# A hybrid decoder layer on one core: modulation columns summed one turn after their load is issued

## The chip, the core and the metric

The kernel runs on one core of one Trainium2 chip. The metric is the device time of one execution in microseconds (us). Times of before are three runs; a profile of one further execution shows where its time went. The core has TensorE (PE, matrix products), VectorE (DVE), ScalarE (ACT), GpSimd (POOL) and SyncE (SP), which here issues all loads and stores from one queue.

## The reference

One layer on 256 tokens of width 2048, all in 32-bit floats. The condition `c` gives nine modulation vectors of 2048 each, three (shift, scale, gate) for each of three parts:

```python
cond = jax.nn.silu(c)
mod = cond @ ada_w[l] + ada_b[l]
sh1, sc1, gt1, sh2, sc2, gt2, sh3, sc3, gt3 = jnp.split(mod, N_MOD, axis=-1)
h = ada_in(x, norm_g[l, 0], sh1, sc1)
x = x + MACARON_W * gt1[:, None, :] * swiglu(h, ...)
h = ada_in(x, norm_g[l, 1], sh2, sc2)
x = x + gt2[:, None, :] * hybrid_mixer(h, ...)
h = ada_in(x, norm_g[l, 2], sh3, sc3)
x = x + MACARON_W * gt3[:, None, :] * swiglu(h, ...)
```

`ada_in` is an RMS norm, scaled and shifted; `swiglu` is two projections to 5632 (gate and up), a product, and one projection down. The mixer projects to eight heads of forgetting attention (FoX) and eight heads of a gated delta rule (GDN) with a short convolution and a triangular solve in chunks of 64, and projects back. A final RMS norm ends the layer.

## The kernel before

**Weights.** All matrices lie in memory as tiles of 128 x 128 in the order in which they are used, eight tiles to a *weight block* of 512 KB; there are 674 blocks. `Stream.next` (L103 on) hands out one tile after the other. At each new block `Stream.block` issues its load (L94, tile `wraw`) and a cast on ScalarE to a shortened format (L96, `whi`, "cast" below); `next` then subtracts on VectorE what the cast kept (L108, `wlo`, "split" below). TensorE multiplies with both. `wraw`, `whi` and `wlo` have three buffers each (L125 to L127); inside the two feed-forward parts every fourth block has one of its own. Blocks 0 to 263 are the first feed-forward part, 264 on the mixer, the last 264 the second feed-forward part. In the mixer blocks 264 to 271 are a first group of projections, 272 to 281 the keys K3 to K7 of the GDN heads (two blocks each), 282 to 289 the gate projection Z0 (`pv`, L717 to L719), 290 to 293 the first GDN head.

**Modulation columns.** The modulation is not computed by TensorE. A column is 128 of its 9 x 2048 outputs: there are 144, and their order is `ada_seq` (shift and scale of the first part in turns, then the other seven vectors). A column's weights, 128 x 2048 floats or 1 MB, are loaded into one of two `adat` buffers (L128, L226), then multiplied with `cs`, the condition, and summed along the row by one VectorE instruction (L228). The first columns have buffers of their own. `ada_col` does both for the next column.

**When a column has its turn.** `next` adds a pace (`RATE`, columns per block, by block number) to an account at each block and calls `ada_col` as `side` whenever it holds one: every third block or so first, every second from block 112, every fourth from 280, every eighth from 408. In the last columns of a feed-forward part `W.quiet` stops the account: the last turn before the mixer comes at block 257 (column 97), the next at block 272. `ada_need` calls `ada_col` out of turn when a column is about to be used. The load is put behind the newest weight load in SP's queue (`tc.issue_after(W.last)`), the sum not ahead of the instruction that `W.behind(False)` names, after a norm its last step.

**The order.** The source says what depends on what; a list scheduler of the framework then lays out each engine's instructions at build time, by readiness in its own reckoning of time and by place in the source. So the order in the source is not always that on the engine. On the chip each engine takes its instructions in that order, and waits at one whose semaphores aren't there.

**The mixer's start.** `keys` (L860) transposes and squares the keys of a head (`pk`, L868; `pkk`, L871; squares, L874; `kk`, L856 and L875) and completes its part of `Ln` (L881), which `decays` (L831) has started with an exponential (L840). `conv_silu` is the short convolution (`cv`, L853 on ScalarE, L855 on VectorE). `solve` (L883) stores the diagonal blocks of `Ln` of four heads in eight small transfers (`ld`, L896), reads them back in another layout (L903) and solves them in a scan of small VectorE steps (L909, L910). All these transfers are in SP's queue, too.

Of the kernel before, what the change touches and what calls it, by code (L numbers as in the profile page):

```python
# [19 lines left out]
KD = D // P  # L20
# [21 lines left out]

HS = 2 * 256 + 64
PAD = {"hs": 16, "w": 56, "hid": 16, "more": 56}
GAP = {"k": 1.0, "gdn": 1.0, "fox": 1.2, "out": 1.0}
ORDER = ("K3 K4 K5 K6 K7 Z0 G0 V0 F0 G1 F1 G2 F2 G3 F3 V1 Z1 G4 F4 G5 F5 G6 G7 F6 F7").split()
N_O = 17
# [23 lines left out]
class Stream:  # L71
# [17 lines left out]
    def block(self, b):  # L89

        raw, hi, lo = self.more if self.more and b % 4 == 3 else (self.raw, self.hi, self.lo)
        pad = 0 if raw is self.raw else PAD["more"]
        r = raw.tile([P, pad + WB * P], F32, name="wraw")[:, pad:]
# [26 lines left out]
def layer_kernel(ctx: ExitStack, tc: tile.TileContext, xrow, c, adaw, cols, cst, w, out, order, dbg=None):  # L120
# [73 lines left out]
    def L(name, lo_=0, n=None):  # L194
        o, wd = COL[name]
        return colt[:, o + lo_ : o + (wd if n is None else lo_ + n)]

    ident = L("ident")

    mod = keep.tile([P, 9 * KD + PAD["hs"]], F32, name="mod")  # L200
    ada_seq = [(m, j) for j in range(KD) for m in (1, 0)]
    for m in (2, 3, 4, 5, 6, 7, 8):
        ada_seq += [(m, j) for j in range(KD)]
    ada_st = {"i": 0}
    ada_done = {}

    def ada_col():

        i = ada_st["i"]
        if i >= len(ada_seq):  # L210
            return
        ada_st["i"] += 1
        m, j = ada_seq[i]
        q = m * KD + j
        if first_ada:
            t = first_ada.pop(0)
            if i >= 2:
                with tc.issue_after(W.last):
                    nc.sync.dma_start(t, adaw[i])
        else:  # L220
            t = adap.tile([P, D], F32, name="adat")
            if W.last is None:
                nc.sync.dma_start(t, adaw[i])
            else:
                with tc.issue_after(W.last):
                    nc.sync.dma_start(t, adaw[i])  # L226
        with W.behind(False):
            V.tensor_tensor_reduce(t, t, cs, 1.0, L("adab", q, 1), ALU.mult, ALU.add, mod[:, q : q + 1])  # L228
        if (m, j) in ada_done:
            ada_done[m, j]()  # L230

    def ada_need(m, j):

        while ada_st["i"] < ada_seq.index((m, j)) + 1:
            ada_col()

    W.side = ada_col

# [71 lines left out]

    hsf = keep.tile([P, KD * HS + PAD["w"]], F32R, name="hs")
    hs = hsf[:, : KD * HS].rearrange("p (k i) -> p k i", k=KD)
# [22 lines left out]
    def modulate(which, m_sh, m_sc):  # L335
        ada_need(max(m_sh, m_sc), KD - 1)
        g1 = gains(which, m_sc, 0, KD)
        r = norm_row(norm_sums())
        hq["next"], hq["one"] = 0, lambda j: modulate_one(
            j, g1[:, j : j + 1], mod[:, m_sh * KD + j : m_sh * KD + j + 1], r)  # L340

    class Early:
# [6 lines left out]
        def y(self, j):  # L349

            ada_need(self.m_sc, j)
            ada_need(self.m_sh, KD - 1)
            if j == 0:
                sh = mod[:, self.m_sh * KD : (self.m_sh + 1) * KD]
                A.copy(hs[:, :, 2 * T], sh)
                V.tensor_sub(hs[:, :, 2 * T + 1], sh, hs[:, :, 2 * T].bitcast(F32))
            g = gains(self.which, self.m_sc, j, 1)
            A.activation(hs[:, j, HI], x[:, j], AF.Copy, scale=g)
            V.scalar_tensor_tensor(hs[:, j, LO], x[:, j], g, hs[:, j, HI].bitcast(F32), ALU.mult, ALU.subtract)
# [45 lines left out]
    def advance(kind):  # L405

        gap = next(chains[kind][0][1], None)
        if gap is None:
            chains[kind].pop(0)
            gap = 0.0  # L410
        due[kind] = clock["now"] + gap * GAP[kind]

# [11 lines left out]
    def start(kind, h, chain):  # L424
        if not chains[kind]:
            due[kind] = clock["now"] + GAP[kind]
        chains[kind].append((h, chain))
# [174 lines left out]
    for kind, i in (("x", 0), ("x", 1), ("c", 0), ("c", 1), ("x", 2), ("x", 3), ("c", 2), ("c", 3)):  # L602
        with nullcontext() if hold is None else tc.issue_after(hold):
            if kind == "c":
                hold = cond(i)
            else:
                t, q = divmod(i, 2)
# [15 lines left out]
    def first_col(i, q):  # L623

        hf = slice(q * D // 2, (q + 1) * D // 2)
        m, j = ada_seq[i]
        col = m * KD + j
        part = ep.tile([P, 1], F32, name=f"part{i}")
        t = first_ada[i][:, hf]
        parts[i] = V.tensor_tensor_reduce(t, t, cs[:, hf], 1.0, L("adab", col, 1) if q == 0 else parts_[i], ALU.mult, ALU.add,  # L630
                                          part if q == 0 else mod[:, col : col + 1]).ins
        if q == 0:
            parts_[i] = part
        return parts[i]
# [18 lines left out]
    first_col(0, 1)  # L653
    first_col(1, 0)
    first_col(1, 1)
    ada_st["i"] = 2
    del first_ada[:2]
    early.close()
    norm2 = Early(2, 6, 7)
# [5 lines left out]
    def mixer():  # L665
# [68 lines left out]
        def gates(ps):  # L734
# [3 lines left out]
            y, ny, e, em, t0, q = (x[:, j, : 2 * GR].rearrange("p (t r) -> p t r", t=2) for j in range(10, KD))  # L738
            coef = tiny.tile([P, GR + PAD["hid"]], F32, name="coef", bufs=1)[:, :GR]
            tc.keep_in_program_order(A.activation(coef, L("alog"), AF.Exp))  # L740
# [595 lines left out]
```

## Time and profile before

| | |
|---|---|
| runs, median of three | 2045.04 us (2044.18 to 2047.87) |
| profiled execution, its own time | 2045.02 us |
| its span | 2043.2 us |
| granted clock of TensorE | 0.992 |
| read from memory | 512.89 MB |
| column loads and sums of 1 MB (L226, L228) | 140 |

The rows of the page's parts and of the waits that matter stand in the prediction. A row of a group reads: line, engine, operation, what it writes and reads, how often; then its busy time and mean duration; then the idle time of the engine ahead of it and what ended that. A row of the timeline reads: start, duration, engine, line, operation, tiles, how often; then, in brackets, the engine's idle time ahead of it and what ended it. A row of the waits reads: who waited for whom, in all, how often, the longest. A row by stretch reads: stretch, length, busy time (and instructions) of TensorE, its weight load, VectorE, ScalarE and GpSimd, then the granted clock, the share of the DMA engines and GB/s.

### The profile page before, as it was taken

To read this page: it belongs to the slowest core of one execution; us is meant where nothing else is said; L and a number is where in the kernel's file an instruction comes from. 1 tells how busy PE (TensorE), PEld (TensorE's weight loads), DVE (VectorE), ACT (ScalarE), POOL (GpSimd) and SP (SyncE) were. 2 spreads that over 40 slices of the span, in tenths; PEclk is the share of its full clock that TensorE was granted. 3 is DMA by queue.
4 is the path that set the end of the run, shared out by engine and by line. 5 is a ranking of instruction groups with operands and counts; after the bars stand their busy time and mean duration, and the time that the engine had idled before them with its cause. 6 is when DMAs were issued, how large, how long until landed. Compare 5 with 4: busy or idle time off the path is not lost.

```text
span 2043.2 us, 33631 instructions
## 1 busy us (share of the span) xinstructions
PE 1997.0 (98%) x13059; PEld 1817.5 (89%) x13059; DVE 1567.2 (77%) x2424; ACT 1023.9 (50%) x1607; POOL 64.7 (3%) x60
## 2 busy tenths in 40 slices
PE   8999999999999998999999999999999999999997
PEld 6999999888888888889989988988888888888886
DVE  6898978889888988889878889876666555555555
ACT  6544544333444447666655654655443344444442
POOL 0000000000000120000000002000000000000012
PEclk8999999999999999999999999999999999999998
DMA  9989767999889885667576657677776555555553
GB/s 344 353 331 327 276 217 269 364 353 368 336 330 341 329 309 177 249 234 247 193 261 213 214 214 294 227 236 242 232 246 217 187 192 189 192 190 190 192 187 113
DMA packets 129489, 519.56 MB, mean 254 GB/s; under 512 B 18217, under 2 KB 21545, under 8 KB 111153
## 3 DMA queue, kind: packets, MB, share of 16 engines
q1 hardware_dynamic: 129330, 517.42, 71.6%
q8 instruction: 102, 1.67, 0.3%
q14 instruction: 57, 0.47, 0.1%
HBM read 512.89 MB, written 4.47 MB: 253 GB/s over the span
## 4 chain that ended last, share of the span: by engine, by line
PE 85%; DVE 7%; DMA 3%; ACT 2%; issue 2%; SPq 0%; DVEq 0%; ACTq 0%
PE pd L434 15%; PE pg L430 10%; PE pu L430 10%; PE pd L435 8%; PE pu L431 5%; PE pg L431 5%; PE pgu L518 5%; PE pgu L517 5%; PE pgu L516 5%; PE po L434 2%; PE pp L704 2%; PE pp L706 2%; PE pp L705 2%; DVE wlo L108 2%; DMA adat<-in_ada_dram 2%
## 5 line engine op out<-in xcount | busy, mean ns | idle before, releaser
L108 DVE TENSOR_TENSOR wlo<-wraw,whi 128x1024 fp32r<-128x1024 f32 x674 | 822.5, 1228 | 306.0 <-ACT whi L96 304.5
L96 ACT CAST whi<-wraw 128x1024 fp32r<-128x1024 f32 x674 | 704.1, 1052 | 624.4 <-issue 153.2
L434 PE MATMUL pd<-hid,whi 128*128 128x512 f32 x1408 | 488.5, 390 | 0.0
L435 PE MATMUL pd<-hid,wlo 128*128 128x256 f32 x1408 | 397.3, 282 | 1.0 <-DVE wlo L108 0.8
L228 DVE CUSTOM_DVE_ANT_0 adat<-adat,cs,colt 128x2048 f32<-128x2048 f32 x140 | 329.4, 2353 | 36.7 <-DMA adat<-in_ada_dram 36.6
L430 PE MATMUL pg<-hs,whi 128*128 128x512 f32 x912 | 318.9, 390 | 0.5 <-DVE shc L382 0.3
L430 PE MATMUL pu<-hs,whi 128*128 128x512 f32 x912 | 318.7, 390 | 0.0
L434 PEld LDWEIGHTS pd<-hid,whi 128*128 128x128 f32 x1408 | 264.1, 188 | 55.0
L435 PEld LDWEIGHTS pd<-hid,wlo 128*128 128x128 f32 x1408 | 266.1, 189 | 3.0 <-DVE wlo L108 2.7
L431 PE MATMUL pu<-hs,wlo 128*128 128x256 f32 x912 | 257.2, 282 | 0.0
L431 PE MATMUL pg<-hs,wlo 128*128 128x256 f32 x912 | 257.2, 282 | 0.0
L516 PE MATMUL pgu<-hs,whi 128*128 128x256 f32 x896 | 248.6, 280 | 7.0 <-ACT hs L321 5.8
L518 PE MATMUL pgu<-hs,wlo 128*128 128x256 f32 x896 | 247.7, 280 | 1.9 <-DVE wlo L108 1.8
L517 PE MATMUL pgu<-hs,whi 128*128 128x256 f32 x896 | 249.6, 280 | 0.0
L430 PEld LDWEIGHTS pg<-hs,whi 128*128 128x128 f32 x912 | 171.1, 188 | 36.8 <-ACT shc L381 0.5
L430 PEld LDWEIGHTS pu<-hs,whi 128*128 128x128 f32 x912 | 171.1, 188 | 35.6
L704 PE MATMUL pp<-hs,whi 128*128 128x256 f32 x656 | 189.5, 290 | 5.6 <-DVE cv L855 2.0
L706 PE MATMUL pp<-hs,wlo 128*128 128x256 f32 x656 | 186.3, 285 | 0.5 <-DVE wlo L108 0.5
L705 PE MATMUL pp<-hs,whi 128*128 128x256 f32 x656 | 185.7, 283 | 0.0
L516 PEld LDWEIGHTS pgu<-hs,whi 128*128 128x128 f32 x896 | 168.4, 189 | 7.9 <-ACT hs L321 6.2
L431 PEld LDWEIGHTS pu<-hs,wlo 128*128 128x128 f32 x912 | 172.3, 189 | 0.3
L431 PEld LDWEIGHTS pg<-hs,wlo 128*128 128x128 f32 x912 | 172.3, 189 | 0.0
(334 smaller groups left out, 2572.6 us busy)
## 6 DMA issues: line engine op xcount, KB each, us to landing
wraw<-in_w_dram SPq DMA_DIRECT2D x674, 512.0 KB, 4.3
adat<-in_ada_dram SPq DMA_DIRECT2D x140, 1024.0 KB, 7.2
xr<-in_xr_dram SPq DMA_DIRECT2D x4, 512.0 KB, 6.1
adaf<-in_ada_dram SPq DMA_DIRECT2D x4, 512.0 KB, 8.2
adaf<-in_ada_dram SPq DMA_DIRECT2D x2, 1024.0 KB, 12.0
xd<-x SPq DMA_DIRECT2D x4, 512.0 KB, 8.4
rw<-rowd SPq DMA_DIRECT2D x16, 128.0 KB, 6.9
x<-xd SPq DMA_DIRECT2D x4, 512.0 KB, 8.5
```

Source lines behind the costliest of these rows:

```text
L96: self.cast = self.nc.scalar.copy(self.h, r).ins
L108: nc.vector.tensor_tensor(self.l, r, self.h.bitcast(F32), ALU.subtract)
L228: V.tensor_tensor_reduce(t, t, cs, 1.0, L("adab", q, 1), ALU.mult, ALU.add, mod[:, q : q + 1])
L430: PE.matmul(ps, wt[0], hs[:, k, ALL], start=(k == 0), stop=False)
L431: PE.matmul(ps[:, T:], wt[1], hs[:, k, HI], start=False, stop=(k == KD - 1))
L434: PE.matmul(ps, wt[0], act.rearrange("p a t -> p (a t)"), start=first, stop=False)
L435: PE.matmul(ps[:, :T], wt[1], act[:, 0], start=False, stop=last)
L516: PE.matmul(o, wh, hs[:, k, HI], start=first and s == 0, stop=False, skip_group_check=skip)
L517: PE.matmul(o, wh, hs[:, k, LO], start=False, stop=False, skip_group_check=skip)
L518: PE.matmul(o, wl, hs[:, k, HI], start=False, stop=last, skip_group_check=skip)
L704: PE.matmul(pp[i][:, :T], wh, hs[:, k, HI], start=(k == 0), stop=False)
L706: PE.matmul(pp[i][:, :T], wl, hs[:, k, HI], start=False, stop=(k == KD - 1))
```

## The change

`ada_col` is split in two: `ada_load` issues a column's load and notes it in `ada_due`; `ada_sum` does the sum. Up to column 15 the sum follows its load at once, as before; from column 16 on one column is left in `ada_due`, so that the turn that issues the load of column i sums column i - 1. The last turn sums all that is left. `ada_need` sums out of turn what is needed.

```diff
+N_PROMPT, ADA_LAG = 16, 1
...
-    ada_st = {"i": 0}
+    ada_st = {"i": 0, "done": 0}
+    ada_due = []
...
     def ada_col():
         i = ada_st["i"]
-        if i >= len(ada_seq):
-            return
-        ada_st["i"] += 1
-        m, j = ada_seq[i]
-        q = m * KD + j
+        if i < len(ada_seq):
+            ada_st["i"] += 1
+            ada_load(i)
+        while len(ada_due) > (ADA_LAG if N_PROMPT <= i < len(ada_seq) else 0):
+            ada_sum(*ada_due.pop(0))
+
+    def ada_load(i):
         if first_ada:
...
                 with tc.issue_after(W.last):
                     nc.sync.dma_start(t, adaw[i])
+        ada_due.append((i, t))
+
+    def ada_sum(i, t):
+        ada_st["done"] = i + 1
+        m, j = ada_seq[i]
+        q = m * KD + j
         with W.behind(False):
             V.tensor_tensor_reduce(t, t, cs, 1.0, L("adab", q, 1), ALU.mult, ALU.add, mod[:, q : q + 1])
...
     def ada_need(m, j):
-        while ada_st["i"] < ada_seq.index((m, j)) + 1:
+        n = ada_seq.index((m, j)) + 1
+        while ada_st["i"] < n:
             ada_col()
+        while ada_st["done"] < n:
+            ada_sum(*ada_due.pop(0))
```

More of the change, by code (lines that the diff above doesn't have):

```diff
@@ L655, in layer_kernel @@
     first_col(1, 1)
-    ada_st["i"] = 2
+    ada_st["i"] = ada_st["done"] = 2
     del first_ada[:2]
```

## The prediction

> **What bounds the kernel now.** I read the page first, then the waits, then busy time by stretch. From the page, parts 1 and 5:
>
> ```profile
> PE 1997.0 (98%) x13059; PEld 1817.5 (89%) x13059; DVE 1567.2 (77%) x2424; ACT 1023.9 (50%) x1607; POOL 64.7 (3%) x60
> L228 DVE CUSTOM_DVE_ANT_0 adat<-adat,cs,colt 128x2048 f32<-128x2048 f32 x140 | 329.4, 2353 | 36.7 <-DMA adat<-in_ada_dram 36.6
> ```
>
> TensorE is busy for 1997.0 of the 2043.2 us of the span, so no change that leaves its work alone can win more than 46 us. The column sums are 140 rows of 2.35 us on VectorE, which waited 36.6 us for their loads. From the waits, VectorE's and the queue's own:
>
> ```profile
> DVE adat L228 <- DMA adat<-in_ada_dram: 36.6, 23, 2.9
> SPq L226 <- DVE mod L228: 61.4, 26, 5.4
> ```
>
> So 23 sums stood on VectorE until their load had landed, 2.9 us at the longest, and 26 column loads stood in SP's queue until an earlier sum freed one of the two buffers. Whether any of it matters is read from TensorE's busy time by stretch:
>
> ```profile
> 90.00:240.00 150.00, 146.60 (x1249) 145.78 (x1248) 139.85 (x178) 66.92 (x83) 0.00 (x0) 1.00 0.89 321
> 357.00:765.00 408.00, 407.01 (x2341) 359.51 (x2340) 361.66 (x421) 175.29 (x225) 19.86 (x12) 1.00 0.91 341
> 765.00:900.00 135.00, 126.51 (x852) 113.75 (x851) 111.34 (x246) 94.01 (x180) 4.32 (x11) 0.97 0.64 228
> 1296.00:1345.00 49.00, 48.46 (x365) 46.08 (x364) 43.81 (x83) 32.98 (x60) 0.00 (x0) 1.00 0.63 217
> 1377.00:2027.00 650.00, 650.00 (x3752) 576.25 (x3751) 387.49 (x494) 292.80 (x397) 18.26 (x14) 1.00 0.60 199
> ```
>
> The first two numbers are the stretch and its length, the third is TensorE. Down-projection and the rest of the first block (357 to 765) lose 1.0 us, the second block from 1377 on nothing. The start of the mixer (765 to 900) loses 8.5 us. A wait of VectorE outside that stretch is covered by TensorE's queue of prepared weights; taking it away buys nothing.
>
> **The change part by part.** It adds no instruction and removes none. I compared the order of each engine in the two built programs. Since a list scheduler places the sums, the lag in the source is not a lag in the program: the sums of nearly all columns stand at the same place on VectorE as before, to the instruction. The engines' orders, and the semaphore values they wait for, differ in three stretches only, around weight blocks 26 to 66, 257 to 297 and 418 to 421.
>
> In **blocks 26 to 66** (90 to 240 us) column 16's sum goes behind three weight splits. Three splits come earlier, the next ones hardly later, and column 16 itself isn't multiplied before block 56. The blocks of lead hide the move; without them one split, 1.2 us, would show. I take 0, between -0.3 and +1.2. In **blocks 418 to 421** (inside 1296 to 1345) column 132's sum goes behind some ten small steps. TensorE loses 0.5 us there in all; I take 0 again, between -0.5 and +0.5.
>
> **Blocks 257 to 297** are the case. Column 97 is issued behind block 257; then no turn comes until block 272, so its sum moves there, from 750 to some 796 us. There VectorE has idle time and the sum itself costs nothing. But the scheduler lays out everything after it anew. In the built order, cut to what follows (numbers are weight blocks; "split" is wlo, L108):
>
> ```
> TensorE before: 272 x24 | 273 x24 | 274 x2 | pk0 pkk0 ...           281 | 282 first half | pk4 pkk4 | 282 ...
> TensorE after:  272 x24 | 273 x2 | 274 x2 | pk0 pkk0 pk1 | 273 x22  281 | pk4 pkk4 | 282 ...
> ScalarE before: cast 282, Exp table, Ln x8, Silu table, kk6, squares, kk3, cv7, cast 283
> ScalarE after:  Exp table, Ln x8, kk2, Silu table, kk6, squares, kk3, cv7, cast 282, cast 283
> VectorE after:  ... cv7, rsa_k, split 282 ... split 285, sum 100, six scan steps (L909, L910), split 286
> SP before:      W285, A100, ld x8, W286, W287, x<-ld, W288      (W, A: loads of weights, of a column)
> SP after:       ld x8, W285, A100, x<-ld, W286, W287, W288
> ```
>
> *First stall, pk0.* Timeline of before: TensorE, ScalarE, VectorE.
>
> ```profile
> 802.12 0.38 PE L704 MATMUL pp<-hs,whi 128*128 128x256 f32 x1 [1.01 <-ACT x L737]
> ...
> 808.50 0.38 PE L868 MATMUL pk<-colt,kk 128*128 128x128 f32 x2
> 806.94 0.73 ACT L856 ACTIVATE kk<-cv 128x256 f32<-128x256 f32 x2
> 807.02 1.22 DVE L108 TENSOR_TENSOR wlo<-wraw,whi 128x1024 fp32r<-128x1024 f32 x1
> ```
>
> ScalarE's order is unchanged up to kk0 and kk1, which end at 807.4 and 807.7. TensorE starts block 272 at 802.12; at 0.12 us a product (rows below) its 24 products, a small transpose and the four early ones of 273 and 274 take it to about 805.8. It now has to stand until 807.4 for pk0, 1.6 us, where before it ran the 22 products of block 273. They need the split of 273, which goes behind the small convolution and gate steps that stood before the split of 274 here (807.02), so it ends near 807.7, in time. With one of two later waits for splits saved (0.5 us together, below): about 1.3 us late.
>
> *Second stall, block 282.*
>
> ```profile
> 831.38 1.08 ACT L96 CAST whi<-wraw 128x1024 fp32r<-128x1024 f32 x1
> ...
> 838.62 0.50 ACT L853 ACTIVATE cv<-pp,colt 128x256 f32<-128x256 f32 x1
> 838.99 2.01 ACT L96 CAST whi<-wraw 128x1024 fp32r<-128x1024 f32 x2
> 837.11 0.28 PE L706 MATMUL pp<-hs,wlo 128*128 128x256 f32 x1
> 837.23 0.39 PE L717 MATMUL pv<-whi,hs 128*128 128x512 f32 x1
> ...
> 840.01 0.38 PE L868 MATMUL pk<-colt,kk 128*128 128x128 f32 x2
> ```
>
> Block 282's cast stood at 831.38, six us ahead of TensorE's first use at 837.23. It now stands behind cv7 (838.62 before), which itself needs the last product of block 281. With the chain ahead of it unchanged in length, cv7 starts near 838.7, the cast ends at about 840.2 and the split, 1.2 us, at 841.5. TensorE, 1.3 us late, is through 281 and the pk4 pair (0.6 us, before inside block 282) at 838.5, can use the cast for two products (0.47 us) and waits for the split. Equivalent start: 841.1, before 837.23 + 0.6 = 837.8. It is now 3.3 us late.
>
> *Third stall, block 286.* SP's queue, VectorE, ScalarE, TensorE of before:
>
> ```profile
> 834.29 0.33 SPq L94 DMA_DIRECT2D wraw<-in_w_dram  x1
> 834.66 0.43 SPq L226 DMA_DIRECT2D adat<-in_ada_dram  x1
> 839.86 4.40 SPq L896 DMA_DIRECT2D ld<-Ln  x8
> 844.36 0.85 SPq L94 DMA_DIRECT2D wraw<-in_w_dram  x2
> 844.82 2.35 DVE L228 CUSTOM_DVE_ANT_0 adat<-adat,cs,colt 128x2048 f32<-128x2048 f32 x1
> ...
> 848.85 1.23 DVE L108 TENSOR_TENSOR wlo<-wraw,whi 128x1024 fp32r<-128x1024 f32 x1 [1.11 <-ACT whi L96]
> 849.99 0.14 DVE L909 TENSOR_TENSOR x<-x 64x1 f32<-64x1 f32 x1
> 850.17 0.15 DVE L910 TENSOR_REDUCE x<-x 64x1 f32<-64x1 f32 x1
> 847.76 1.05 ACT L96 CAST whi<-wraw 128x1024 fp32r<-128x1024 f32 x1 [3.63 <-DMA wraw<-in_w_dram]
> 850.12 0.50 PE L718 MATMUL pv<-wlo,hs 128*128 128x512 f32 x1 [0.17 <-DVE x L909]
> ```
>
> The eight small stores wait for the last Ln (839.86) and hold SP for 4.4 us. Block 285 and column 100 were issued ahead of them, at 834.29 and 834.66; now they go behind, at 844.3 and 844.7. A block issued at 844.36 was cast at 847.76, the moment it had landed, so 285 lands 3.4 us after issue at 847.8, is cast by 848.9 and split by 850.1. The column's megabyte follows at the 341 GB/s of the busy stretch, 3.1 us, and lands at 850.8. Sum 100 runs from then to 853.1, six scan steps of 0.18 us to 854.2, and only then comes the split of 286, done by 855.4. TensorE used it at 850.12: 5.3 us late. This holds whatever the first two stalls cost (TensorE is there by 853), so it is not added to them; it takes them in. The next blocks come from buffers that these splits free, three of each, so they shift alike; I take 0.2 us back at block 290, where TensorE waited anyway.
>
> [...]
>
> Bounds for the third stall: the page's landing row below has 7.2 us as the median of a column's load.
>
> ```profile
> adat<-in_ada_dram SPq DMA_DIRECT2D x140, 1024.0 KB, 7.2
> ```
>
> Landing 7.2 us after 844.7 puts the lag at 6.4; landing before split 285 is done at 850.1 puts it at 4.6. The stores themselves may come 1.3 us earlier or later with the Ln chain. That is 3 to 8 us.
>
> **Sum**, against the profiled execution's own 2045.02 us (1.8 us outside the span of 2043.2; it agrees with the median of the runs, 2045.04): 0 + 5.3 - 0.2 + 0 = +5.1, so 2050.1; I say 2050.0.
>
> **The rivals.** *Taken back later* (not slower). TensorE's waits from 765 to 867 and, behind the dots, from 867 to 1224:
>
> ```profile
> PE pp L704 <- ACT whi L96: 1.4, 2, 1.0
> PE pp L706 <- DVE wlo L108: 0.5, 2, 0.3
> ...
> PE pp L704 <- DVE cv L855: 2.0, 1, 2.0
> PE pv L717 <- DVE cv L855: 1.0, 1, 1.0
> ```
>
> If these end on chains that keep their time while TensorE is late, such as row fetches and the solve's round trip to memory, the lag vanishes there. For it: the solve's scan feeds all heads, and VectorE's convolution steps (cv) queue behind it. Against it: cv starts from what TensorE has just computed, and loads follow freed buffers. It decides if the 3.0 us of cv waits have a releaser that is on time: 2050 - 3.0 = 2047, and with block 291's 1.4 and a shorter third stall (3.3) 2043.6. I give it 2043 to 2049, middle 2046.
>
> *Longer chain.* The late blocks of the V and G projections meet more column loads in SP's queue, and each block of lost lead costs again: a second stall like the third, +10 or more, 2052 to 2060.
>
> *The sums do lag.* If sums stood a turn later after all, two buffers would be one too few from 357 us on: a load lands in 7.2 us, the block behind it 1.5 later (its half megabyte at 341 GB/s), cast, split and sum take 1.05 + 1.2 + 2.35, so two turns take 13.3 us. TensorE needs 407.0 us / 2341 = 0.174 us a product, 16 a block, two blocks a turn: 11.1 us. Over the 28 turns of blocks 112 to 168 that is 28 x 1.1 = +31 us, 2076. [...] The built order speaks against it.
>
> *A real gain* would need TensorE's 8.5 us of the mixer's start back; I see no place where the new order gives more than 1.
>
> **How the numbers follow.** 0.2% of 2045 is 4.1 us, about what a measurement of this kernel can tell from no change. Forecast (2047.5 to 2056): 0.56, of which 0.07 lies under 2049.1. Taken back: 0.31. Longer chain: 0.07. Lag: 0.02. Gain: 0.04. Faster 0.04; within 0.2%: 0.31 + 0.07 = 0.38; slower 0.58. The range leaves out the gain, the lag, half the longer chain and the lowest third of "taken back": 2044.5 to 2056.
>
> **What the new profile would show.** Unchanged stretches: TensorE at 407 us of 408 before the mixer and without a gap from 1377 on, VectorE's waits for column loads much as they were. A TensorE wait of about 1.6 us on ScalarE's kk near 806, one on a split near 841, one on a split near 855, block 285's load issued behind the eight stores, and from 870 on everything 5 us later. I am wrong if sums stand on VectorE without ever waiting for a load, if the eight stores go out much before 838, or if the lag at 870 is gone at 1300.

## The result and the profile after

The changed kernel takes 2052.7 us (median of 15 runs, 2049.37 to 2056.91), the kernel before, on the same chip, 2046.61 us (15 runs, 2043.04 to 2051.54). The ratio is 1.0025, with a 95% interval of 1.0017 to 1.0033: some 5.1 us slower, between 3.5 and 6.8 (the two medians alone lie 6.1 apart). The profiled execution took 2051.48 us with a span of 2049.7 (before: 2045.02 and 2043.2).

From the page after, engines and the group of the column sums; then the waits of VectorE and of SP's queue (total, times, longest, in us):

```profile
PE 2000.1 (98%) x13058; PEld 1819.5 (89%) x13059; DVE 1567.5 (76%) x2424; ACT 1021.5 (50%) x1607; POOL 63.4 (3%) x60
...
L239 DVE CUSTOM_DVE_ANT_0 adat<-adat,cs,colt 128x2048 f32<-128x2048 f32 x140 | 329.3, 2352 | 30.0 <-DMA adat<-in_ada_dram 29.9
```

```profile
DVE adat L239 <- DMA adat<-in_ada_dram: 29.9, 21, 2.9
```

```profile
SPq L231 <- DVE mod L239: 63.7, 27, 5.4
```

21 sums still stand until their load has landed (before 23), 27 loads still wait for an earlier sum (before 26). So a change that says "sum one turn later" has left these waits nearly as they were. Busy time by stretch, after:

```profile
357.00:765.00 408.00, 407.01 (x2341) 359.53 (x2340) 357.73 (x419) 175.09 (x225) 19.14 (x13) 1.00 0.91 341
765.00:900.00 135.00, 122.19 (x814) 109.40 (x812) 108.78 (x236) 89.29 (x165) 3.57 (x10) 0.97 0.60 212
...
1377.00:2027.00 650.00, 650.00 (x3752) 576.25 (x3751) 390.48 (x495) 294.53 (x401) 17.52 (x13) 1.00 0.62 202
```

TensorE loses the same 1.0 us between 357 and 765, nothing from 1377 on, and 12.8 us instead of 8.5 at the mixer's start. Its timeline there, with the idle time ahead of an instruction and its releaser in brackets:

```profile
807.22 0.44 PE L882 MATMUL pk<-colt,kk 128*128 128x128 f32 x2 [1.23 <-ACT kk L870]
...
840.75 0.73 PE L731 MATMUL pv<-whi,hs 128*128 128x512 f32 x2 [0.60 <-ACT whi L98]
842.17 0.50 PE L732 MATMUL pv<-wlo,hs 128*128 128x512 f32 x1 [0.69 <-DVE wlo L110]
...
851.02 0.50 PE L732 MATMUL pv<-wlo,hs 128*128 128x512 f32 x1 [0.43 <-DVE wlo L110]
...
855.83 0.50 PE L732 MATMUL pv<-wlo,hs 128*128 128x512 f32 x1 [1.23 <-DVE wlo L110]
```

These are the first stall at 807, the second at 840.75 and 842.17, the third at 851 and 855.83. Before, the only wait at one of these places is 0.17 us, at 850.12. What makes the third one, in SP's queue and on VectorE:

```profile
840.51 4.47 SPq L910 DMA_DIRECT2D ld<-Ln  x8
845.08 0.38 SPq L96 DMA_DIRECT2D wraw<-in_w_dram  x1
845.50 0.43 SPq L231 DMA_DIRECT2D adat<-in_ada_dram  x1
```

```profile
849.75 1.23 DVE L110 TENSOR_TENSOR wlo<-wraw,whi 128x1024 fp32r<-128x1024 f32 x1 [3.72 <-ACT whi L98]
851.26 2.35 DVE L239 CUSTOM_DVE_ANT_0 adat<-adat,cs,colt 128x2048 f32<-128x2048 f32 x1 [0.29 <-DMA adat<-in_ada_dram]
...
854.55 1.23 DVE L110 TENSOR_TENSOR wlo<-wraw,whi 128x1024 fp32r<-128x1024 f32 x1
```

The load of block 285 (845.08) stands behind the eight stores, column 100's sum behind its load (851.26), and the split of 286 behind both: done at 855.77, where TensorE used it at 850.12 before.

### The profile page after: what moved, and what is told of

Read it like the earlier page. It is cut to its first block, busy times and chain, and to the rows that moved or that the text cites. A ratio compares the mean times of both kernels' runs of the same rounds, so it can differ in the third digit from the quotient of the medians.

```text
span 2049.7 us, 33637 instructions
## 1 busy us (share of the span) xinstructions
PE 2000.1 (98%) x13058; PEld 1819.5 (89%) x13059; DVE 1567.5 (76%) x2424; ACT 1021.5 (50%) x1607; POOL 63.4 (3%) x60
## 3 DMA queue, kind: packets, MB, share of 16 engines
q8 instruction: 102, 1.67, 0.3%
## 4 chain that ended last, share of the span: by engine, by line
PE 86%; DVE 6%; DMA 3%; ACT 3%; issue 2%; SPq 0%; DVEq 0%; ACTq 0%
PE pd L448 15%; PE pg L444 10%; PE pu L444 10%; PE pd L449 8%; PE pu L445 5%; PE pg L445 5%; PE pgu L532 5%; PE pgu L530 5%; PE pgu L531 5%; PE po L448 2%; PE pp L718 2%; PE pp L720 2%; PE pp L719 2%; DVE wlo L110 2%; DMA adat<-in_ada_dram 1%
```

## The experiments

The totals need a second measure beside them. In the programs that are the same up to block 255 (the kernel before and five of the kernels below), the cast of block 96 starts between 293.6 and 301.1 us in the profiled executions: 7.5 us of scatter before anything differs. So each trace is also read from the start of ScalarE's cast of block 256 to that of block 308, which takes in the mixer's start and nothing else. The rows for before, then after, two casts of 1.0 us in a group where it says x2:

```profile
744.71 1.99 ACT L96 CAST whi<-wraw 128x1024 fp32r<-128x1024 f32 x2
...
921.18 1.05 ACT L96 CAST whi<-wraw 128x1024 fp32r<-128x1024 f32 x1
```

```profile
744.33 1.99 ACT L98 CAST whi<-wraw 128x1024 fp32r<-128x1024 f32 x2
...
927.46 1.05 ACT L98 CAST whi<-wraw 128x1024 fp32r<-128x1024 f32 x1
```

That is 176.5 us before and 183.1 after: +6.65 in this one execution. A stretch is read from one execution of each kernel, so it has scatter of its own: the kernel before with its stores off SP has the orders of before up to block 280 and is 1.57 us faster there. All kernels by both measures (us = ratio less 1, times 2047; the line numbers of the experiments lie a few lines off):

| kernel | ratio (95%) | us | blocks 256 to 308 |
|---|---|---|---|
| changed | 1.0025 (1.0017 to 1.0033) | +5.1 | +6.65 |
| changed, again | 1.0023 (1.0013 to 1.0033) | +4.7 | +5.12 |
| all but column 97 | 0.9995 (0.9982 to 1.0007) | -1.0 | -0.35 |
| only column 97 | 1.0040 (1.0027 to 1.0052) | +8.2 | +10.10 |
| 97 and 98 held | 1.0017 (1.0008 to 1.0026) | +3.5 | +3.07 |
| SP's order alone (third stall) | 1.0035 (1.0023 to 1.0048) | +7.2 | +4.77 |
| cast of 282 late (second and third) | 1.0033 (1.0019 to 1.0048) | +6.8 | +5.38 |
| changed, stores off SP | 1.0025 (1.0012 to 1.0038) | +5.1 | +6.27 |
| before, stores off SP | 1.0016 (1.0003 to 1.0028) | +3.3 | +0.14 |
| first stall alone | 1.0002 (0.9989 to 1.0014) | +0.4 | +4.33 |

**Which column.** Two kernels part the change in two:

```diff
-        while len(ada_due) > (ADA_LAG if N_PROMPT <= i < len(ada_seq) else 0):
+        while len(ada_due) > (ADA_LAG if N_PROMPT <= i < len(ada_seq) and i != 97 else 0):
```

> The changed kernel, except that column 97 is summed in the turn that issues its load, as before. In the built order blocks 26 to 66 and 418 to 421 stand as in the changed kernel, blocks 257 to 297 as before. Theory (the price is the new layout of blocks 257 to 297 and nothing else): the time of before, 2046.6, within 1.0 us; lag of the casts behind before within 0.5 us everywhere. Rival A (the other two stretches or the lag as such cost something): 2048 to 2052, with a lag that appears by block 70 or at block 420. Rival B (5 us are scatter of the runs): no forecast of its own; then this kernel and the next one differ by less than 1 us.

```diff
-        while len(ada_due) > (ADA_LAG if N_PROMPT <= i < len(ada_seq) else 0):
+        while len(ada_due) > (ADA_LAG if i == 97 else 0):
```

> The kernel before, with column 97 alone summed one turn later. In the built order only blocks 257 to 297 differ from before, and they stand as in the changed kernel. Theory: all of the price, 2046.6 + 5.1 = 2051.7 (2050 to 2053.5), lag 0 until block 260, 1 to 1.5 at 272, some 6 from block 296 on. Rival A: less than half of it, under 2049. Rival B: as the kernel without column 97's delay.

Without column 97's delay nothing is left of the price (-1.0, between -3.7 and +1.4; -0.35 in the stretch). With it alone the whole price is there, rather more than expected: +8.2, between 5.5 and 10.6. The two differ by 9 us, so this is no scatter. Why its trace has 10.1 us where the changed kernel, which has the same order there, has 6.65 is told by the granted clock (the third number from the end). After, then only column 97:

```profile
800.00:810.00 10.00, 8.77 (x73) 8.37 (x72) 9.28 (x21) 9.35 (x16) 0.00 (x0) 1.00 0.36 129
820.00:830.00 10.00, 10.00 (x88) 10.00 (x87) 7.29 (x12) 6.42 (x11) 0.00 (x0) 1.00 0.90 331
```

```profile
800.00:810.00 10.00, 8.18 (x56) 7.70 (x55) 7.83 (x20) 6.09 (x9) 0.00 (x0) 0.83 0.42 164
820.00:830.00 10.00, 9.23 (x66) 8.86 (x67) 6.08 (x18) 6.90 (x11) 0.00 (x0) 0.83 0.70 237
```

At 0.83 over 10 us, 1.7 us of clock are lost, twice. An estimate without them is 10.1 less 3.4, or 6.7.

**Does a later sum cost by itself?** Columns 97 and 98 held behind the split of the next turn by an order that the scheduler must keep:

```diff
-        while len(ada_due) > (ADA_LAG if N_PROMPT <= i < len(ada_seq) else 0):
+        while len(ada_due) > (ADA_LAG if i in (97,98) else 0):
...
-        with W.behind(False):
+        with tc.issue_after(W.split) if i in (97,98) else W.behind(False):
             V.tensor_tensor_reduce(...)
```

> Columns 97 and 98 alone are held behind the split of the next turn. Column 97's sum stands behind block 272 as in the changed kernel, but TensorE's order in blocks 272 to 280 and SP's whole order stay those of before; a few small moves are left in blocks 281 to 286. Theory (not the later sum but the order that the scheduler lays out behind it costs, and most of it hangs on SP's order): the time of before, 2046.6, within 1.5 us. Rival A (a sum one turn later costs by itself): 2050 to 2052.

Column 97's sum now stands behind block 272 as in the changed kernel, and blocks 272 to 280 keep TensorE's order of before. From the cast of 256 to that of 280 this trace is 0.24 us behind before: the later sum is free to within the scatter. 2.83 of the 3.07 us come after 280, where small moves are left. SP's queue of this trace, 8.0 us behind the one of before when the mixer starts:

```profile
847.27 0.33 SPq L96 DMA_DIRECT2D wraw<-in_w_dram  x1
847.65 0.43 SPq L231 DMA_DIRECT2D adat<-in_ada_dram  x1
849.34 5.29 SPq L910 DMA_DIRECT2D ld<-Ln  x8
854.72 0.85 SPq L96 DMA_DIRECT2D wraw<-in_w_dram  x2
```

The order is that of before, but the stores end later, and block 286 behind them goes out 2.4 us later than before (854.72 less 8.0 is 846.7, before 844.36). My expectation of no cost was wrong, and the time of 2050.73 lies where rival A put it; but the trace has the cost behind block 280, not at the later sum, and the split of 286 is 2.4 us late like its load behind the stores.

**The stalls one by one.** The third alone, then the second and third, both made from the kernel before:

```diff
+        with self.tc.issue_after(self.ld) if b == 285 else nullcontext():
             self.last = self.nc.sync.dma_start(r, self.w[b]).ins
...
```

> The kernel before, with the load of block 285 held behind the eight small stores (ld) in SP's queue; column 100's load follows it. Blocks 257 to 284 and every column's sum stand as before; from block 285 on the orders are those of the changed kernel. This is the third stall alone. Theory (the third stall takes in the earlier two): block 285 issued some 10 us later, split 286 the late one, casts 5 to 6 us late from block 290 on, 2051.7 (2050 to 2053.5). Rival (the stalls add up, the third alone is what is left of the changed kernel's 6.5 us after 3.3): 3 us, 2049 to 2050.

```diff
+        with self.tc.issue_after(self.cv) if b == 282 else nullcontext():
             self.cast = self.nc.scalar.copy(self.h, r).ins
...
```

> The kernel before, with ScalarE's cast of block 282 alone held behind the first step of the last key's convolution (cv7). Every column's sum and blocks 257 to 280 stand as before; from block 281 on all orders, SP's among them, are those of the changed kernel. The second and third stall without the first. Theory (the third takes in the second, and the first): split of 282 a gap of 2 to 3 us near 841, split of 286 the last late one, 5 to 6 us late from block 290 on, 2051.7 (2050 to 2053.5), the same as the kernel with SP's order alone within 1 us. Rival (they add): 2 to 3 us more than the kernel with SP's order alone.

4.77 and 5.38 us in the stretch, +7.2 and +6.8 in time: by the time the third stall alone gives as much as all three, though intervals of 4.7 to 9.8 and 3.9 to 9.8 can't tell 1 or 2 us. The traces say more, once the stretch is cut at the cast of block 280, which lies behind the first stall and ahead of the other two (us against before):

| kernel | 256 to 280 | 280 to 308 |
|---|---|---|
| changed | +1.88 | +4.77 |
| changed, again | +0.22 | +4.91 |
| only column 97 (3.4 of clock in the first) | +4.82 | +5.28 |
| third stall alone | +0.20 | +4.57 |
| second and third | -0.04 | +5.42 |

Behind block 280 the third stall alone gives what the second and third give together, to within 0.9 us: the third takes in the second. What these traces have lost up to block 280 is still there at block 308, on top of it: the first stall is not taken in. In the five traces that have it, 0.2 to 2.8 us stand at block 280 (1.4 with column 97 alone, less its clock), in the six without it (the kernels with the real lag below left out) between -1.6 and +0.2. SP's queue with the third alone, then TensorE:

```profile
840.67 4.07 SPq L897 DMA_DIRECT2D ld<-Ln  x8
844.84 0.38 SPq L95 DMA_DIRECT2D wraw<-in_w_dram  x1
```

```profile
849.29 0.74 PE L718 MATMUL pv<-whi,hs 128*128 128x512 f32 x2 [1.56 <-ACT whi L97]
850.55 0.50 PE L719 MATMUL pv<-wlo,hs 128*128 128x512 f32 x1 [0.52 <-DVE wlo L109]
...
853.79 0.73 PE L718 MATMUL pv<-whi,hs 128*128 128x512 f32 x2 [0.64 <-ACT whi L97]
855.76 0.60 PE L719 MATMUL pv<-wlo,hs 128*128 128x512 f32 x1 [1.23 <-DVE wlo L109]
```

TensorE comes to block 285 unhindered and pays there what it had paid at the second stall in the changed kernel (1.56 and 0.64 on casts are new). It goes on 110.4 us after its cast of block 256, the changed kernel 111.5 and in its second trace 109.9, the kernel before at 105.4. The kernel with the late cast also shows where SP's new order comes from:

```profile
840.44 4.68 SPq L897 DMA_DIRECT2D ld<-Ln  x8
845.22 0.37 SPq L94 DMA_DIRECT2D wraw<-in_w_dram  x1
```

With one cast moved and nothing else, the scheduler put block 285, and column 100 with it, behind the stores by itself; the buffer for 285's load comes free with the split of 282.

**Is it SP's queue alone?** The eight stores and the load that brings them back on GpSimd's queue, in the changed kernel and in the kernel before:

```diff
-                    nc.sync.dma_start(ld[ht, b]...
+                    (nc.sync if half else nc.gpsimd).dma_start(ld[ht, b]...
...
-                nc.sync.dma_start(blk, ld[ht]...
+                (nc.sync if half else nc.gpsimd).dma_start(blk, ld[ht]...
```

> The changed kernel, with the first half's eight small stores and the load that fetches them back (ld, x<-ld) on GpSimd's queue, so that block 285 and column 100 do not stand behind them. TensorE, VectorE and ScalarE keep the changed kernel's order up to block 285. Theory: the third stall is gone, the first two are left: casts 2.5 to 4 us late from block 290 on, 2049 to 2050.5. Rival A (SP's order is not what costs): 2051 to 2053, as the changed kernel. Rival B (a stall leaves TensorE at half clock for 3.4 us in some executions, 1.7 us each): the profiled run may show one or two more of these than before, and the time lies up to 2 us higher than the gaps tell.

> The kernel before with the same edit: the control for the kernel that has the stores of the changed kernel on GpSimd's queue. TensorE loses nothing between 805 and 860 in the kernel before, so moving the stores away gives it nothing: 2046.6 within 1.0. If the stores in SP's queue cost the kernel before something too (blocks 286 and 287 stand behind them), up to 1.5 us faster, and then gaps at 865 and 877 are shorter.

The changed kernel gains nothing by it (+5.1, and 6.27 in the stretch): the 2.5 to 4 us that I expected did not come, and rival A was right in its number. SP's queue, VectorE, ScalarE and TensorE of the changed kernel with the stores away:

```profile
835.58 8.20 SPq L96 DMA_DIRECT2D wraw<-in_w_dram  x2
843.83 0.43 SPq L231 DMA_DIRECT2D adat<-in_ada_dram  x1
```

```profile
842.21 1.22 DVE L110 TENSOR_TENSOR wlo<-wraw,whi 128x1024 fp32r<-128x1024 f32 x1
...
851.28 2.35 DVE L239 CUSTOM_DVE_ANT_0 adat<-adat,cs,colt 128x2048 f32<-128x2048 f32 x1 [0.31 <-DMA adat<-in_ada_dram]
...
855.35 0.15 DVE L923 TENSOR_TENSOR x<-x 64x1 f32<-64x1 f32 x1 [1.71 <-DMA x<-ld]
...
855.79 1.22 DVE L110 TENSOR_TENSOR wlo<-wraw,whi 128x1024 fp32r<-128x1024 f32 x1
```

```profile
848.66 1.05 ACT L98 CAST whi<-wraw 128x1024 fp32r<-128x1024 f32 x1 [2.57 <-DMA wraw<-in_w_dram]
```

```profile
857.07 0.49 PE L732 MATMUL pv<-wlo,hs 128*128 128x512 f32 x1 [2.37 <-DVE x L924]
```

The second load of the first row, block 285's, ends at 843.78: it had to wait for the split of 282, done at 843.43, which frees its buffer. So it is out only 1.7 us earlier than behind the stores (845.46). Even that is not kept: its cast starts at 848.66, as in the changed kernel, since the load took 5.2 us from its issue (843.43) where it had taken 3.6 (from 845.08); what slowed it was not shown. And the edit made a wait of its own: the scan steps wait 1.71 us for the load that brings the stored blocks back, and the split of 286 stands behind these steps. TensorE's third stall is here one wait of 2.37 us on it. So the run doesn't say what the changed kernel would cost with nothing but the stores taken out of the way of block 285. It does show a second condition on that load: the split of 282. In the changed kernel it is done at 842.11, and the stores hold the load 3.0 us longer than that.

The control is 1.57 us faster than before up to block 280, where the orders are the same, and 1.72 slower from there to 308, in all +0.14; so it doesn't show that the edit is free. Its time is 3.3 us up (0.6 to 5.7), where 1.0 at the most was expected. In the trace its cast of block 96 stands at 298.5 us, 4.9 behind that of before, in a part where the programs are the same; whether the other runs started as late isn't recorded.

**The first stall alone.** The changed kernel with the loads and casts of 281 and 282 written ahead of block 280's products, so that the cast of 282 should come early again (the first of block 280's eight weight tiles is another column of the same matrix in it, so its output is not the layer's; the instructions are the same):

```diff
+            if b == 280:
+                for n in range(2):
+                    rl = self.block(b + 1 + n)
+                    self.early.append((rl, self.h))
...
```

> The changed kernel, with the load and cast of blocks 281 and 282 written ahead of block 280's products, so that the scheduler puts the cast of 282 ahead of most of the Ln steps again and block 285 and column 100 ahead of the eight stores in SP's queue, as before. Blocks 272 to 280 stand as in the changed kernel: column 97's sum moved, the first stall, and neither the second nor the third. Theory (the first stall lasts and also pushes the Ln chain): casts 1 to 2.5 us late from block 276 on and still at 300, 2048 to 2049. Rival A (it is taken back where TensorE waits 2.4 us between 865 and 877 in the kernel before): under 0.5 us late at block 300, 2046 to 2047. Rival B (blocks 272 to 280 are what costs): 2051 or more.

> The changed kernel once more, on the chip of the kernel with the first stall alone. 2051.7 (2050 to 2053.5). The gaps of TensorE at 807, 841, 851 and 856 in the same places as in its first profile, split 286 done 5.5 to 6.5 us later than in the kernel before, set against the casts of blocks 256 to 260; stretches of 3.4 us at half clock in other places than in the first profile if these follow from the phase of an execution rather than from the program.

The timed runs say almost nothing is left (+0.4, between -2.3 and +2.9, beside +4.7 of the changed kernel on the same chip), the trace says +4.33 in the stretch (2.83 of it at block 280 already) and +2.6 by the end. Its rows show a first stall as in the changed kernel, and then this queue:

```profile
840.53 0.33 SPq L96 DMA_DIRECT2D wraw<-in_w_dram  x1
840.91 0.43 SPq L240 DMA_DIRECT2D adat<-in_ada_dram  x1
843.13 4.45 SPq L919 DMA_DIRECT2D ld<-Ln  x8
848.27 0.83 SPq L96 DMA_DIRECT2D wraw<-in_w_dram  x2
```

Block 285 goes out ahead of the stores again, but these start 3.3 us later than before (843.13 to 839.86): in its built order ScalarE runs the Ln steps in two groups, with two more table loads (1.28 us each in the traces of before and after). Block 286 stands behind them, as before, and goes out at 848.27 instead of 844.36. Nor is the cast of 282 as early as before: it starts at 838.19, ahead of cv7 but behind the Ln steps (before 831.38, changed 839.64). So this is not the first stall alone. The run doesn't settle what the first stall costs by itself; it lies between 0 and 4 us. What it does show is that with block 285 ahead of the stores again the kernel's time can't be told from before, though the first stall is in it. In the second trace of the changed kernel the split of 286 is done 4.4 us later than before, counted from the cast of block 256, where I had expected 5.5 to 6.5.

**If the sums did lag.** The rival that the built order spoke against, made real: every sum from column 16 on held behind the split of the next turn; then the same with a third buffer for columns until the mixer (no spare hidden tiles, `HIDX0`, in the first block instead of three, and a pad of 40 instead of 56 in the pool `more`); and its control, the same without that buffer.

```diff
-        with W.behind(False):
+        with tc.issue_after(W.split):
             V.tensor_tensor_reduce(...)
```

> Every sum from column 16 on is held behind the weight split of the turn in which the next column's load is issued, so that the lag exists in the built order too, with two column buffers as before; blocks 272 to 286 then keep TensorE's order of before. Rival in the prediction (the sums do lag): two turns take 13.3 us where TensorE has 11.1 in blocks 112 to 168, 28 x 1.1 = +31 us inside the stretch from 357 to 765; in all 2076 to 2085 with up to 8 us for a new layout of blocks 290 to 382. The other possibility (the loads have enough lead, and a sum that stands later only waits less): TensorE at 407 of the 408 us there as before, VectorE's waits for column loads near 0, and a total of 2044 to 2054 by what the later layout costs.

```diff
+HIDX0 = 0
...
-            t = adap.tile([P, D], F32, name="adat")
+            t = (W.adax if W.adax and i % 3 == 2 else adap).tile([P, D], F32, name="adat")
...
```

> The kernel with every sum held one turn, with a third column buffer until the mixer (every third column has it); the room for it is taken from the three spare hidden tiles of the first block. Theory (the lag costs because two buffers make load, cast, split and sum one chain): the 14.2 us that TensorE lost between 357 and 765 with two buffers shrink to 1 to 3, and SP's waits for an earlier sum from 206 us to under 60; total 2050 to 2058. Rival (the sums cost where they stand on VectorE, behind the split): 12 us or more lost there still, 2068 to 2073.

> The control for it: the same kernel without the three spare hidden tiles, but with two column buffers. 12 to 16 us lost between 357 and 765, total 2068 to 2076. If the spare tiles matter themselves, more than 16 lost.

The real lag costs 25.6 us (2071.91; 1.0125, 1.0110 to 1.0140), less than the 2076 to 2085 expected. In turn: busy time between 340 and 540 before; SP's waits for an earlier sum and the same stretch with the real lag, and a column load's median landing from its page; waits and stretch with three buffers.

```profile
340.00:540.00 200.00, 199.01 (x1160) 175.77 (x1159) 177.29 (x204) 77.63 (x86) 0.00 (x0) 1.00 0.95 357
```

```profile
SPq L231 <- DVE mod L239: 206.4, 52, 7.2
```

```profile
340.00:540.00 200.00, 188.05 (x1076) 163.00 (x1076) 167.41 (x188) 70.53 (x74) 0.00 (x0) 0.99 0.86 324
```

```profile
adat<-in_ada_dram SPq DMA_DIRECT2D x140, 1024.0 KB, 5.6
```

```profile
SPq L232 <- DVE mod L240: 56.6, 25, 4.7
```

```profile
340.00:540.00 200.00, 197.94 (x1158) 174.56 (x1157) 177.62 (x203) 78.08 (x85) 0.00 (x0) 1.00 0.95 353
```

From the cast of block 112 to that of 168 the real lag adds 15.2 us, its control 15.7, with a third buffer 0.7. The control ran once (2076.28), so its total has no interval. The mechanism was right: the chain of load, cast, split and sum through two buffers. The kernel with three buffers is still 1.0038 (1.0024 to 1.0052) of before; of its trace, 9.5 us come at the mixer's start, where it has two buffers and sums that are held, 4.4 are won back by block 408, and 2.8 come in the second block (cast of 408 to that of 660), where its control has them too.

## Why the prediction was right, point by point

- **The bound** held: 407.01 us between 357 and 765 to the hundredth, no gap from 1377 on, and the price in the one stretch with waits.
- **Three stretches, two of them free.** Shown by the pair of kernels around column 97. Blocks 26 to 66 and 418 to 421 cost -1.0 us (-3.7 to +1.4), taken as 0.
- **First stall.** Predicted 1.6 us on kk near 806 and TensorE 1.3 us late; measured 1.23 at 807.22, and the cast of block 280, behind it, 1.9 us late in one trace and 0.2 in the other, of which 1.4 and 0.5 stand at block 272, ahead of the stall. Not foreseen: 0.66 us at 816.87 on the gates' transposed products (prow).
- **Second stall.** Cast of 282 done at 840.69 (predicted 840.2), split at 842.11 (841.5).
- **Third stall.** The numbers came as worked out, each 0.4 to 0.9 us late: 285 issued at 845.08 (844.3), its split done at 850.97 (850.1), column 100's sum from 851.26 (850.8), split of 286 done at 855.77 (855.4). Put on the clock of before by the cast of block 256, the two traces of the changed kernel have this split at 856.2 and 854.5, so the prediction lies between them.
- **"It takes them in"** held for the second stall (4.57 us behind block 280 with the third alone, 5.42 with both) and not for the first. The working kept the end of the Ln steps, and with it the stores, where they were before, whatever TensorE had lost. But these steps start from TensorE's products: with column 97 alone, 4.82 us late at block 280, the stores start 4.0 us late and the split of 286 9.6. So the first stall is a term that was put at nothing, and the traces have 0.2 and 1.9 us for what stands at block 280 in its place. That +5.1 was forecast and +5.1 measured is luck in part: the price behind block 280 is 4.8 to 4.9 us in the changed kernel's traces, and the rest is smaller than their scatter.
- **The step that was incomplete** is the third stall's cause. "Now they go behind" names SP's stores alone. The late split of 282 holds the load of 285 too, until 842.11, and it is why the scheduler put that load behind the stores: the second stall is not merely covered by the third, the moved cast is the root of both. With the stores out of SP's queue I expected 2.5 to 4 us of lag; there were 6.3, but that edit made the solve's load late as well, so how much of them is due to the split of 282 stays open.
- **"0.2 us back at block 290"** was wrong in sign: TensorE's three waits there are 1.95 us after (0.57, 0.93, 0.45) against 1.67 before (0.26, 0.96, 0.45). Small.
- **Rivals.** Taken back later: no; from block 308 to 408 the changed kernel wins 0.4 us in one trace and loses 1.9 in the other. Longer chain: not in the changed kernel's traces. Real lag: not in the changed kernel, and mis-sized, 15 us where +31 was worked out. Its terms: a load lands in 5.6 us (median of all columns with the lag; 4.7 at the least), not 7.2, at a DMA share of 0.86 between 340 and 540 (before 0.95), and why it lands sooner was not traced; and two turns took 11.7 us before (27 turns in 158.1 us), not 11.1. With the lag they take 12.7 (27 turns in 171.8 us), which is 1 to 2 us more than the chain adds up to with these landings (5.6 or 4.7 + 1.5 + 1.05 + 1.2 + 2.35); what fills the rest was not traced.
- **A term that was missing**: the half clock behind some of TensorE's waits (below; 0.83 over 10 us, twice, with column 97 alone). It did not move the median of the changed kernel beyond the range, but it makes single traces differ by up to 3.4 us.

## What to carry to other kernels

Where a scheduler orders the instructions, compare the built orders first: here the delay of all columns but one cost nothing that could be measured, and that of one made the scheduler move a cast, which moved a queue, which delayed a load that the splits and TensorE stood behind. Ask of a late transfer for every condition that it waits for, its place in the queue and its buffer. Before you read "no gain" off an edit that takes one of them away, look in its trace for the wait that the edit put in its place. A wait later on takes in an earlier one only if what ends it doesn't start from the late engine. And where runs scatter by more than the effect, measure the stretch in which the programs differ, from one instruction to another, beside the total.

## What the runs showed of the hardware

In the traces of before and after, between 30 and 2030 us, TensorE's granted clock falls to one half in pieces of 3.41 or 6.83 us (before: 32.59 to 36.00 and 773.28 to 780.11), each behind 1.36 us or more of idle time in the 3.41 us ahead of it. By single microseconds, the granted clock in the trace with column 97 alone is 0.78, 0.50, 0.50, 0.52 from 806 to 810, behind a wait of 1.82 us that ended at 805.22, and 0.81, 0.50, 0.50, 0.50 from 823 to 827, behind 1.34 us of idle time between 819 and 821. Two traces with the same wait, 1.23 us at 855.8, differ: the third stall alone (which has 0.64 us more idle two us earlier), then the changed kernel.

```profile
855.00:860.00 5.00, 4.24 (x12) 3.34 (x13) 4.73 (x14) 1.11 (x2) 0.00 (x0) 0.66 0.67 247
```

```profile
855.00:860.00 5.00, 4.17 (x18) 3.41 (x19) 4.73 (x14) 1.83 (x3) 0.00 (x0) 1.00 0.66 233
```

12 products against 18 in the same 5 us: the busy time hides it, the clock and the count show it. In the 3.4 us ahead of its half clock the first of the two has 0.64 + 1.23 = 1.87 us of idle time, the changed kernel around the same wait (854.24 to 857.66) only the 1.23. No run was made to find which idle times decide; the traces of before and after tell some of it. In each of them these pieces lie on one grid of 3.413 us: before they start at 32.59, 773.28 and 1220.43, which are 217 and 131 steps apart, after at 31.63, 775.74 and 1226.29, 218 and 132 steps. Cut into such steps from 50 to 2030 us, the two traces have three at full clock in which TensorE is idle for more than 1.9 us in all (2.18, 2.21 and 2.45), and half clock follows all three. It follows none of three with 1.5 to 1.9 us, one of ten with 1.0 to 1.5, and none of 1134 with less. One of the three with 1.5 to 1.9, in the trace of before, holds 1.88 us of a wait of 2.03 us that ends at 1114.77 and lies across the edge of two steps. These are too few steps to say how much idle time it takes.

The 1.82 and the 1.34 us with column 97 alone and the 0.64 + 1.23 us with the third stall alone were each followed by 1.7 us of lost clock (0.83 over 10 us, 0.66 over 5), the 1.23 us in the changed kernel by none. What is lost is not always paid: in the trace with the third stall alone the half clock at 856 leaves nothing behind, with splits 5.0 us late at block 286 and 4.7 at 291.

The other thing is the scatter at the start, 293.0 to 301.1 us for the cast of block 96 in the traces here. Its cause was not looked for.
